# Where the weights of half-token products begin: one place, or six in turn

## The chip, the cores and the metric

The kernel runs on one core of a Trainium2 chip. The metric is the device time of one execution in microseconds; of several runs the median counts.

## The reference

Two decoder layers over 512 tokens of width 1024, all in float32. What matters here is the MLP that ends each layer and the gemms around it:

```python
def hybrid_layer(x, g_mix, w_in, sinks, w_a, w_b, w_out, g_mlp, w_up, w_down):
    h = rmsnorm(x, g_mix)
    z = h @ w_in                      # q, k, v, retention and gate columns
    ...                               # windowed attention and retention
    mixed = jax.nn.sigmoid(ga) * ya + jax.nn.sigmoid(gb) * yb
    x = x + mixed @ w_out
    h2 = rmsnorm(x, g_mlp)
    x = x + jnp.square(jax.nn.relu(h2 @ w_up)) @ w_down      # D_FF = 4096
    return x

def reference(x, ...):
    for l in range(DEPTH):            # DEPTH = 2
        x = hybrid_layer(x, ...)
    return rmsnorm(x, g_final)
```

## The kernel before, in words

Everything is kept transposed: features on the 128 partitions, tokens along the free dimension. Each float32 operand is split in two rounded parts, high and low, and each product of a weight block with an activation tile is three matmuls that accumulate in PSUM (`products`, L282 to L284): high weights on high activations, high weights on low activations, low weights on high activations. The weights are the stationary operand, a block of 128 x 128; the activations are the moving operand, 512 columns for all the tokens or 256 for half of them. Each matmul has a weight load of its own, so the same high block is loaded twice.

The weights come from HBM in units of 128 x 1024 floats (eight blocks of 128 columns), in an order written out by hand (`unit_order`). `split_until` takes the next unit, has ScalarE round it to the high part (L237) and VectorE subtract to get the low part (L238), both into rotating buffers of the pool `wpool`, three deep. `unit` hands out a unit and keeps the splitting three units ahead. A buffer is 1024 + 128 floats long, that is 4608 bytes or nine times 512, so all buffers begin at the same remainder of 512 bytes, and so do the activation tiles. A weight block is 512 bytes per partition.

Most gemms use all 512 tokens. Two parts use half the tokens:

- The `pair` steps of the up projection. Two chunks of 128 features are computed together by a scheme of seven products in place of eight (the blocks are halves of the contraction and halves of the tokens). A pair has four parts, which VectorE forms by adding and subtracting halves of the loaded weights (`add_part`); seven calls of `multiply` then do four blocks each on 256 columns. There are 14 pairs per layer, and their entry in the order is `("pair", j, part)` with j = 4, 6, ... 30. Between two pairs stands a `down` step: two output chunks of the down projection over all 512 tokens. A layer's sequence is `first`, two pairs, then twelve times down and pair, then `last`.
- The last gemm of the second layer (`end`), which goes twice over the same eight units of `w_down`, once per half of the tokens. The first three units come from `wpool`; the last five are split into `homes`, tiles of the slots named r, where they begin at the start of the tile.

The profile names operands by tile: a matmul `mm<-r,hi` has the moving operand r and the weights hi; `mm<-r,r` and `mm<-uhi,r` of 256 columns are the matmuls of `end` with weights in `homes`.

For units of half-token products (the pairs, and the last eight units of all) the weights begin `ASIDE` = 48 floats into the buffer, which is 192 bytes; for all other units they begin at its start:

```python
first = ASIDE if paired or i >= len(order) - 8 else 0
hi, lo = (wpool.tile([P, UNIT + P], F32R, tag=n, name=n)[:, first : first + UNIT] for n in ("hi", "lo"))
```

Of the kernel before, what the change touches and what calls it, by code (L numbers as in the profile page):

```python
# [46 lines left out]
PACE = 0.8  # L47
DEEP = 3
DELAY = 2
ASIDE = 48  # L50


def unit_order():

    order = [("w_in", i) for i in range(4 + 2 + 8 + 2 + 4 + 2)]
    order += [("w_in", i) for i in range(22, 26)]
    order += [("w_a", i) for i in range(4)]
    order += [("w_in", i) for i in range(26, 42)]
    order += [("w_b", i) for i in range(4)]
    order += [("w_in", i) for i in range(42, 46)]  # L60
    order += [("w_b", i) for i in range(4, 8)]
    order += [("w_out", i) for i in range(8)]
    for what, q, i in mlp_sequence():
        if what == "first":
            order += [("w_up", u) for u in range(4)]
        elif what == "pair":
            order += [("pair", 8 * q + 2 * i, part) for part in range(4)]
        elif what == "down":
            order += [("w_down", 8 * q + 2 * i + u) for u in range(2)]
        else:  # L70
            order += [("w_down", 8 * q + u) for u in range(8)]
    return order
# [43 lines left out]
def decoder(ctx, tc, xT, x_first, w_in, w_a, w_b, w_out, w_up, w_down, tables, decay, band, out):  # L116
# [11 lines left out]
    def f32(ap):  # L128
        return ap.bitcast(F32)
# [25 lines left out]
    order = [(layer, *u) for layer in range(DEPTH) for u in unit_order()]  # L155
# [3 lines left out]
    def halves(i):  # L159

        return (slice(0, UNIT // 2), slice(UNIT // 2, UNIT)) if i < 3 else (slice(0, UNIT),)
# [11 lines left out]
    def load_until(n):  # L173
        while state["loaded"] < min(n, len(order)):
            i = state["loaded"]
            layer, name, j = order[i][:3]
            if name == "pair":
                load_part(i)
            else:
                raws[i] = raw_tile()  # L180
                for at in halves(i):
                    queue = nc.scalar if i == 0 and at.start == 0 else nc.sync
                    queue.dma_start(raws[i][:, at], weights[name][layer, j][:, at])
                    if i < 3:
                        load_x()
            state["loaded"] += 1
# [17 lines left out]
    def add_part(i):  # L204
        part = order[i][3]
        if part == 0:
            w2 = raws[i + 3]
            nc.vector.tensor_tensor(raws[i][:, RIGHT], w2[:, RIGHT], w2[:, LEFT], ALU.add)
        elif part == 1:
            w1 = raws[i - 1]  # L210
            nc.vector.tensor_tensor(raws[i][:, LEFT], w1[:, RIGHT], w1[:, LEFT], ALU.subtract)
        elif part == 2:
            raws[i] = big("raw3").rearrange("p a t -> p (a t)")
            w1, w2, z2 = raws[i - 2], raws[i + 1], raws[i - 1]
            nc.vector.tensor_tensor(raws[i][:, LEFT], w1[:, LEFT], w2[:, RIGHT], ALU.subtract)
            nc.vector.tensor_tensor(raws[i][:, RIGHT], z2[:, RIGHT], z2[:, LEFT], ALU.subtract)

    def split_until(n):
        while state["split"] < min(n, len(order)):
            i = state["split"]  # L220
            load_until(i + 3)
            paired = order[i][1] == "pair"
            if paired:
                add_part(i)
            raw = raws[i]
            if homes and i >= len(order) - len(homes):
                home = homes[len(order) - 1 - i]
                hi, lo = (home[:, 2 * a : 2 * a + 2, :].rearrange("p a t -> p (a t)") for a in range(2))
            else:

                first = ASIDE if paired or i >= len(order) - 8 else 0
                hi, lo = (wpool.tile([P, UNIT + P], F32R, tag=n, name=n)[:, first : first + UNIT] for n in ("hi", "lo"))
            for at in (LEFT,) if paired and order[i][3] == 3 else halves(i):
                if i == 0 and at.start == 0:
                    nc.vector.tensor_copy(hi[:, at], raw[:, at])
                else:
                    nc.scalar.activation(hi[:, at], raw[:, at], AF.Copy)  # L237
                nc.vector.tensor_tensor(lo[:, at], raw[:, at], f32(hi[:, at]), ALU.subtract)  # L238
            raws.pop(i - 3 if paired else i, None)
            parts[i] = (hi, lo)  # L240
            state["split"] += 1

    def unit(name, layer):
        i = state["next"]
        assert order[i][:2] == (layer, name), (order[i], layer, name)
        state["next"] += 1
        split_until(i + 3)
        return parts.pop(i)
# [851 lines left out]

    scaled_input(0, 0)
    split_until(1)
    for u in (2, 3):
        for k in (2 * u - 3, 2 * u - 2):
            scaled_input(k, 0)
        split_until(u)
# [149 lines left out]
```

## Time and profile before

| | |
|---|---|
| median of 3 runs | 1505.11 us (1504.9 to 1505.15) |
| the profiled execution | 1507.24 us |
| its span, first to last instruction | 1505.5 us |
| mean granted TensorE clock | 0.998 |
| matmuls, TensorE busy | 8080, 1493.5 us (99%) |
| weight loads, busy | 8080, 1297.2 us (86%) |
| VectorE, ScalarE busy | 1026.4 us (68%), 740.1 us (49%) |
| HBM traffic over the span | 100 GB/s |

The half-token stages lie at 436 to 710 us (pairs of the first layer, with the down steps between them), 1178 to 1438 us (pairs of the second layer) and 1438 us to the end (`end`). A row of the groups of instructions reads: line, engine, operation, out<-in, stationary size, shape and count | busy us, mean ns of one | idle time before. A row of the timeline reads: start us, length us, engine, line, operation. The duration of a matmul holds the latency of the pipeline; matmuls overlap, so the step from one start to the next is shorter than a duration.

### The profile page before, as it was taken

The page shows a single profiled execution, that of the slowest core. Times are in us where ns is not written, and L with a number is a line of the kernel's source. Part 1 is how long each engine was busy: PE and PEld are TensorE (multiplying, and loading weights), DVE is VectorE, ACT ScalarE, POOL GpSimd, SP SyncE. Part 2 cuts the span into 40 slices and gives each one's busy share as a digit, 9 for nine tenths or more (in the row PEclk, how much of TensorE's full clock was granted, in tenths as well). Part 3 has the DMA queues.
Part 4 walks back from the last instruction along what each step waited for, and adds up shares of the span by engine and source line. Part 5 has one row for each costly group of instructions (what it writes and reads, how often), then busy time and mean ns, then how long its engine had stood idle before and what let it go on. Part 6 is the DMA issues. An engine that isn't in the chain of part 4 may idle for free.

```text
span 1505.5 us, 20498 instructions
## 1 busy us (share of the span) xinstructions
PE 1493.5 (99%) x8080; PEld 1297.2 (86%) x8080; DVE 1026.4 (68%) x1598; ACT 740.1 (49%) x1163; POOL 2.9 (0%) x13
## 2 busy tenths in 40 slices
PE   9999999999999999999999999999999999999997
PEld 7888888888888999989888888888888999899997
DVE  6877658754697666676678765677449866666664
ACT  6656455632564444444455643555226544444452
POOL 0000000000000000000000000000000000000000
PEclk9999999999999999999999999999999999999999
DMA  6322322233223232233442222222342222232231
GB/s 215 125 99 71 95 87 91 71 126 125 98 73 112 99 111 88 98 111 115 166 130 94 85 84 89 81 90 84 126 126 91 92 98 98 99 109 101 100 111 57
DMA packets 52640, 155.10 MB, mean 103 GB/s; under 512 B 6208, under 2 KB 8384, under 8 KB 52544
## 3 DMA queue, kind: packets, MB, share of 16 engines
q1 hardware_dynamic: 52400, 153.54, 30.5%
q8 instruction: 63, 1.03, 0.3%
q14 instruction: 33, 0.27, 0.1%
q10 hardware_dynamic: 144, 0.26, 0.0%
HBM read 146.96 MB, written 4.19 MB: 100 GB/s over the span
## 4 chain that ended last, share of the span: by engine, by line
PE 98%; ACT 1%; DVE 0%; DMA 0%; issue 0%; DVEq 0%
PE mm L284 29%; PE mm L282 29%; PE mm L283 29%; PE rv L282 2%; PE rv L284 2%; PE rv L283 2%; PE score L653 1%; PE pT L618 1%; PE r L283 1%; PE r L284 1%; PE r L282 1%; PE pv L639 0%; PE pv L638 0%; PE ssq L376 0%; PE ret L283 0%; PE ret L284 0%
## 5 line engine op out<-in xcount | busy, mean ns | idle before, releaser
L237 ACT ACTIVATE hi<-raw 128x1024 fp32r<-128x1024 f32 (+1 forms) x313 | 314.7, 1013 | 514.0 <-PE mm L283 430.7
L238 DVE TENSOR_TENSOR lo<-raw,hi 128x1024 fp32r<-128x1024 f32 (+1 forms) x314 | 362.6, 1164 | 161.7 <-ACT hi L237 160.7
L283 PE MATMUL mm<-r,hi 128*128 128x512 f32 (+1 forms) x1136 | 390.2, 344 | 0.0
L282 PE MATMUL mm<-r,hi 128*128 128x512 f32 (+1 forms) x1136 | 387.8, 345 | 1.1 <-ACT mm L1039 1.1
L284 PE MATMUL mm<-r,lo 128*128 128x512 f32 (+1 forms) x1136 | 386.7, 344 | 0.0
L282 PE MATMUL mm<-xh,hi 128*128 128x512 f32 (+1 forms) x1008 | 357.0, 356 | 0.6 <-ACT xh L292 0.6
L283 PE MATMUL mm<-xl,hi 128*128 128x512 f32 (+1 forms) x1008 | 355.5, 355 | 0.0
L284 PE MATMUL mm<-xh,lo 128*128 128x512 f32 (+1 forms) x1008 | 354.9, 355 | 0.0
L282 PEld LDWEIGHTS mm<-r,hi 128*128 128x128 f32 x1136 | 212.5, 187 | 27.6 <-ACT mm L1039 1.5
L283 PEld LDWEIGHTS mm<-r,hi 128*128 128x128 f32 x1136 | 213.3, 188 | 25.9
L284 PEld LDWEIGHTS mm<-r,lo 128*128 128x128 f32 x1136 | 213.1, 188 | 25.6
L282 PEld LDWEIGHTS mm<-xh,hi 128*128 128x128 f32 x1008 | 189.8, 188 | 26.7 <-ACT xh L292 1.3
L283 PEld LDWEIGHTS mm<-xl,hi 128*128 128x128 f32 x1008 | 190.1, 189 | 25.5
L284 PEld LDWEIGHTS mm<-xh,lo 128*128 128x128 f32 x1008 | 189.9, 188 | 25.6
L1066 DVE TENSOR_TENSOR x<-x,mm 128x512 f32<-128x512 f32 x56 | 37.8, 687 | 33.7 <-PE mm L284 33.7
L284 PE MATMUL rv<-hi,xl 128*128 128x512 f32 x128 | 49.8, 389 | 0.0
L283 PE MATMUL rv<-lo,xh 128*128 128x512 f32 x128 | 49.8, 389 | 0.0
L282 PE MATMUL rv<-hi,xh 128*128 128x512 f32 x128 | 49.4, 391 | 0.0
L283 PE MATMUL mm<-ulo,hi 128*128 128x512 f32 (+1 forms) x128 | 46.1, 362 | 0.0
L282 PE MATMUL mm<-uhi,hi 128*128 128x512 f32 (+1 forms) x128 | 46.1, 362 | 0.0
L284 PE MATMUL mm<-uhi,lo 128*128 128x512 f32 (+1 forms) x128 | 45.5, 363 | 0.0
L1046 DVE SCALAR_TENSOR_TENSOR z<-mm,rstd 128x256 f32<-128x256 f32 x28 | 11.9, 425 | 40.2 <-PE mm L284 40.2
(188 smaller groups left out, 1681.6 us busy)
## 6 DMA issues: line engine op xcount, KB each, us to landing
raw<-w_in_in SPq DMA_DIRECT2D x89, 512.0 KB, 3.3
raw<-w_down_in SPq DMA_DIRECT2D x64, 512.0 KB, 3.3
raw<-w_up_in SPq DMA_DIRECT2D x36, 512.0 KB, 3.3
raw<-w_up_in SPq DMA_DIRECT2D x56, 256.0 KB, 2.8
raw<-w_b_in SPq DMA_DIRECT2D x16, 512.0 KB, 3.2
raw<-w_out_in SPq DMA_DIRECT2D x16, 512.0 KB, 3.6
raw<-w_a_in SPq DMA_DIRECT2D x8, 512.0 KB, 3.3
x<-xT_in SPq DMA_DIRECT2D x15, 256.0 KB, 3.7
```

What stands on the lines that cost most here:

```text
L237: nc.scalar.activation(hi[:, at], raw[:, at], AF.Copy)
L238: nc.vector.tensor_tensor(lo[:, at], raw[:, at], f32(hi[:, at]), ALU.subtract)
L282: nc.tensor.matmul(ps, ah, bh, start=start and i == 0, stop=False, **more)
L283: nc.tensor.matmul(ps, ah, bl, start=False, stop=False, **more)
L284: nc.tensor.matmul(ps, al, bh, start=False, stop=stop and i == n - 1, **more)
L618: nc.tensor.transpose(pt[:, i * P : (i + 1) * P], sm[:, at : at + P], ident)
L653: nc.tensor.matmul(ps[:, g * w : (g + 1) * w], q_s[g][:, c, at], part[:, keys], start=i == 0, stop=i == 1)
L1046: nc.vector.scalar_tensor_tensor(z[:, 0, :H], a, 0.0, rms_mlp.value[:, :H], ALU.max, ALU.mult)
L1066: nc.vector.tensor_tensor(x[:, c, :], x[:, c, :], ps, ALU.add)
```

## The change

The one place of 48 floats becomes a list of six places, 16, 32, 64, 80, 96 and 112 floats (64, 128, 256, 320, 384 and 448 bytes). A pair takes the place by its number, j // 2 modulo six, and all four parts of a pair have the same place; each of the last units takes it by its own number. All other units still begin at the start of the buffer.

```diff
-ASIDE = 48
+ASIDE = (16, 32, 64, 80, 96, 112)
...
-                first = ASIDE if paired or i >= len(order) - 8 else 0
+
+                j = order[i][2]
+                first = ASIDE[(j // 2 if paired else j) % len(ASIDE)] if paired or i >= len(order) - 8 else 0
                 hi, lo = (wpool.tile([P, UNIT + P], F32R, tag=n, name=n)[:, first : first + UNIT] for n in ("hi", "lo"))
```

## The prediction

> **What bounds the kernel now.** I read the page first: its busy shares, then the chain of work that ended last.
>
> ```profile
> PE 1493.5 (99%) x8080; PEld 1297.2 (86%) x8080; DVE 1026.4 (68%) x1598; ACT 740.1 (49%) x1163; POOL 2.9 (0%) x13
> ...
> PE 98%; ACT 1%; DVE 0%; DMA 0%; issue 0%; DVEq 0%
> ```
>
> TensorE is the bound nearly everywhere: 98% of the chain is matmul after matmul. So the time is the number of matmuls times the step from one start to the next, and a change that touches only how a weight load reads its operand is worth what it does to that step. The groups of instructions, with shapes kept apart, come next, because matmuls of 256 columns (half the tokens) are what the change touches.
>
> ```profile
> L282 PE MATMUL mm<-xh,hi 128*128 128x512 f32 x672 | 263.3, 395 | 0.6 <-ACT xh L292 0.6
> ...
> L282 PE MATMUL mm<-r,hi 128*128 128x256 f32 x464 | 129.8, 280 | 1.1 <-ACT mm L1039 1.1
> ...
> L282 PE MATMUL mm<-xh,hi 128*128 128x256 f32 x336 | 93.8, 279 | 0.0
> ...
> L282 PE MATMUL mm<-r,r 128*128 128x256 f32 x48 | 13.6, 283 | 0.0
> ...
> L282 PE MATMUL mm<-uhi,r 128*128 128x256 f32 x32 | 9.1, 283 | 0.0
> ```
>
> The second name on the right is the stationary operand. Weights named "hi" of 256-column matmuls lie 48 floats (192 bytes) into their buffer; weights named "r" are the five units of the last gemm that sit in the slot tiles, at a multiple of 512 bytes from the moving operand (place zero below). The first kind reads 279 to 280 ns, the second 283. The weight loads say the same:
>
> ```profile
> L282 PEld LDWEIGHTS mm<-r,hi 128*128 128x128 f32 x1136 | 212.5, 187 | 27.6 <-ACT mm L1039 1.5
> ...
> L282 PEld LDWEIGHTS mm<-r,r 128*128 128x128 f32 x48 | 9.2, 192 | 0.0
> ```
>
> A load takes 187 ns in one kind and 192 in the other. (The first row mixes half and full matmuls.) A duration holds the pipeline's latency, so the step has to be read from starts. The timeline of TensorE gives it for one uninterrupted stretch of each kind, and the groups in the same stretch give the counts:
>
> ```profile
> 469.22 0.28 PE L282 MATMUL mm<-r,hi 128*128 128x256 f32 x1
> ...
> 476.17 0.28 PE L284 MATMUL mm<-r,lo 128*128 128x256 f32 x1
> ...
> L282 PE MATMUL mm<-r,hi 128*128 128x256 f32 x12 | 3.3, 279 | 0.0
> L283 PE MATMUL mm<-r,hi 128*128 128x256 f32 x12 | 3.3, 279 | 0.0
> L284 PE MATMUL mm<-r,lo 128*128 128x256 f32 x11 | 3.1, 280 | 0.0
> L284 PE MATMUL mm<-xh,lo 128*128 128x256 f32 x8 | 2.2, 280 | 0.0
> L282 PE MATMUL mm<-xh,hi 128*128 128x256 f32 x8 | 2.2, 279 | 0.0
> L283 PE MATMUL mm<-xl,hi 128*128 128x256 f32 x8 | 2.2, 279 | 0.0
> ```
>
> The groups (taken up to 476.1) hold 59 matmuls before the one at 476.17: 6.95 us / 59 = 117.8 ns a step with the weights at 192 bytes.
>
> ```profile
> 1460.73 0.28 PE L284 MATMUL mm<-uhi,r 128*128 128x256 f32 x1
> ...
> 1469.97 0.28 PE L283 MATMUL mm<-ulo,r 128*128 128x256 f32 x1
> ...
> L284 PE MATMUL mm<-uhi,r 128*128 128x256 f32 x14 | 4.0, 283 | 0.0
> L282 PE MATMUL mm<-uhi,r 128*128 128x256 f32 x14 | 4.0, 283 | 0.0
> L283 PE MATMUL mm<-ulo,r 128*128 128x256 f32 x14 | 4.0, 283 | 0.0
> L282 PE MATMUL mm<-r,r 128*128 128x256 f32 x12 | 3.4, 283 | 0.0
> L283 PE MATMUL mm<-r,r 128*128 128x256 f32 x12 | 3.4, 283 | 0.0
> L284 PE MATMUL mm<-r,r 128*128 128x256 f32 x12 | 3.4, 283 | 0.0
> ```
>
> Here 78 matmuls, 77 steps: 9.24 us / 77 = 120.0 ns at place zero. The place of the weights is thus worth 2.2 ns a step between the two places that the trace shows. A third value stands where the last gemm goes from place zero back to weights at 192 bytes:
>
> ```profile
> 1471.17 0.28 PE L284 MATMUL mm<-r,r 128*128 128x256 f32 x1
> 1471.29 0.28 PE L282 MATMUL mm<-r,hi 128*128 128x256 f32 x1
> ...
> 1472.20 0.28 PE L284 MATMUL mm<-r,lo 128*128 128x256 f32 x1
> ...
> L282 PE MATMUL mm<-r,hi 128*128 128x256 f32 x3 | 0.8, 276 | 0.0
> ```
>
> From 1471.29 to 1472.20 are eight steps, 0.91 / 8 = 113.8 ns (the starts are rounded to 10 ns, so 1 ns either way), and these matmuls read 276 ns. The same place has a quicker rhythm than the usual one, and it ended only when another product came between. So there are at least three rhythms: 113.8, 117.8 and 120.0.
>
> **The change part by part.** Nothing is added, removed or moved: every engine issues the same instructions in the same order, and all buffers keep their addresses. What changes is the offset, within its buffer, of the weights of the products with half the tokens. A weight block of 128 floats is 512 bytes, and the moving operands start at multiples of 512 bytes from one another, so one number per unit (its place, 64 to 448 bytes) describes all its blocks.
>
> *Counts.* A pair does seven products of 4 blocks, three matmuls each: 84. There are 14 pairs a layer, numbered 2 to 15, and the number modulo six gives the place; the three buffered units of the last gemm have 2 x 24 matmuls each, at the first three places. That makes 384 at 64 bytes (4 pairs and a unit), 384 at 128, 552 at 256 (6 pairs and a unit), 504 at 320, 336 at 384 and 336 at 448: 2,496 matmuls, all on the path. None remains at 192 bytes.
>
> *The evacuations and splits.* ScalarE (L237) and VectorE (L238) write the units to the new places. The row of L237 in the half-token stage (436 to 710 us, 192 bytes for nearly all) and in the stage ahead of it (250 to 430 us, place zero):
>
> ```profile
> L237 ACT ACTIVATE hi<-raw 128x1024 fp32r<-128x1024 f32 x66 | 68.7, 1058 | 108.7 <-PE mm L283 108.7
> ...
> L237 ACT ACTIVATE hi<-raw 128x1024 fp32r<-128x1024 f32 x31 | 32.8, 1060 | 71.7 <-PE mm L283 54.4 <-issue 17.3
> ...
> 436.00:710.00 274.00, 273.44 (x1765) 249.64 (x1764) 187.58 (x256) 127.33 (x183) 0.96 (x1) 1.00 0.31 104
> ```
>
> 1058 against 1060 ns: the writer does not mind the place, and it waits 108.7 us for TensorE in that stage. I cost this at nothing; the cover is that wait. In the stretch's own row (busy us of PE, PEld, DVE, ACT, POOL, then clock, DMA share) VectorE has 187.58 of 274 us and the DMA engines 0.31, so even 4 ns less a step (3%) makes neither late. The granted clock is 1.00.
>
> *The steps.* Each place costs its matmuls times the difference of its step from 117.8. The trace shows no weights at the six places, so I bound them by its rows: all at 120.0 gives 2,496 x 2.2 = +5.5 us; all at 113.8 gives 2,496 x -4.0 = -10.0 us; all as 192 bytes gives 0. Nothing excludes an end. What I take: the rows show that 120.0 is what the usual layout gives, at two sorts of moving operand and for 9 us on end, and 192 bytes the one place that has escaped it, and that with a margin of only 2.2 ns. I read it as an exception with a width. Its neighbours at 128 and 256 bytes get half the relief: (384 + 552) x 1.1 = 1.0 us. The other four, 384 + 504 + 336 + 336 = 1,560 matmuls, fall back to 120.0: 1,560 x 2.2 = 3.4 us. Sum: +4.5 us. The edges between half and full products (two or so at each of 28 pairs) would at 2.2 ns each add 0.1 us, which I leave out.
>
> [...]
>
> The profiled execution ran 1507.24 us, with a span of 1505.5; 1.7 us lie around the span, and the change leaves those alone. Its sum is 1507.2 + 4.5 = 1511.7. The median of the three runs is 1505.11, 2.1 us below the profiled one, and the steps are the same in kind, so the forecast goes by the median: 1505.1 + 4.5 = 1509.6 us.
>
> **The rivals.**
> *Several places keep the quick rhythm (faster).* [...] For it: the nine matmuls at 1471.29 held it until interrupted. Against: in the stretch at 469.22, entered from full matmuls as every pair is, the same place ran 117.8 from end to end. A place is worth on the mean 416 matmuls x 4.0 = 1.7 us; with two quick and the rest at 117.8 it is -3.3 us (1501.8), three -5.0 (1500.1), all six -10.0 (1495.1). It decides for faster when the mean step falls below 116.6 ns (3.0 us / 2,496 = 1.2 ns).
>
> *The place matters only when it is zero, or by halves (no change).* If only equal starts collide, all six run as 192 bytes does: 1505.1. If only the places nearer to a multiple of 512 than to 192 (64, 384, 448 bytes: 1,056 matmuls) fall back, it is +2.3 us (1507.4). For it: just one bad place is on show. Against: just one better place is, too.
>
> *Worse than zero.* Places close to a multiple of 512 could cost more than zero itself. The nearest dearer row of that shape:
>
> ```profile
> L282 PE MATMUL r<-r,r 128*128 128x256 f32 x16 | 4.6, 290 | 0.0
> ```
>
> That is 7 ns over 283. At 64 and 448 bytes, 720 matmuls x 7 = 5.0 us more: 1514.6. Against: those are short products between others of other lengths, not a steady stream.
>
> **How the numbers follow.** The forecast, +3.3 (six tenths of the matmuls at 120.0) to +5.5 us, has 0.42; worse than zero 0.08; no change or halves 0.25; quick places 0.25. Only the first is my likeliest and gives 1509.6, its own range 1508.4 to 1510.6. With 0.2% being 3.0 us, about what a measurement of this kernel can tell from no change: slower 0.50, same 0.25, faster 0.25. For 8 in 10 the range goes up past all places at 120.0 to 1511.5, leaving most of the dearest case out (0.06), and down to 1500.5, which holds the cases of no change and of two quick places and leaves out three and more (0.13).
>
> **What would show it.** In the profile after, the 256-column matmuls of "hi" and "lo" should read 283 ns and their loads 192 in the pairs at 64, 320, 384 and 448 bytes, and something between in the others; the timeline within a pair should step by 120.0. L237 and L238 stay at their durations and the full matmuls at theirs. The forecast is wrong if pairs at those places read 279 ns (no change) or 276 (faster), or if the pairs do not differ by their number at all; and the mechanism is wrong if the time moves while the 256-column rows do not.

## The result and the profile after

The changed kernel runs 1510.77 us (median of 6 runs), the kernel before 1505.13 beside it: a ratio of 1.0028, 95% interval 1.0017 to 1.0038. The profiled execution took 1511.14 us. One thing has to be known to read single times of this kernel: its first matmuls step by 427 ns and later ones by 227, and how long that lasts differs from run to run, which moves a run by an estimated 2 us (last section), so steps are read from the trace.

The page of the kernel after, span, busy time and the chain that ended last:

```profile
span 1509.4 us, 20498 instructions
...
PE 1497.0 (99%) x8080; PEld 1299.8 (86%) x8080; DVE 1026.3 (68%) x1598; ACT 739.9 (49%) x1163; POOL 2.9 (0%) x13
...
PE 98%; ACT 1%; DVE 0%; DMA 0%; issue 0%; DVEq 0%
```

TensorE still carries 98% of the chain; VectorE and ScalarE are unchanged (1026.4 and 740.1 us busy before, 1026.3 and 739.9 after). The groups of TensorE instructions with shapes kept apart (the lines have moved by two), and L239 of ScalarE, once L237, in the first pair stage:

```profile
L284 PE MATMUL mm<-r,hi 128*128 128x256 f32 x464 | 130.8, 282 | 1.0 <-ACT mm L1041 1.0
...
L284 PE MATMUL mm<-xh,hi 128*128 128x256 f32 x336 | 94.5, 281 | 0.0
...
L284 PE MATMUL mm<-r,r 128*128 128x256 f32 x48 | 13.6, 283 | 0.0
...
L239 ACT ACTIVATE hi<-raw 128x1024 fp32r<-128x1024 f32 x66 | 68.7, 1058 | 109.8 <-PE mm L285 108.0 <-DVE lo L240 1.8
```

The half-token matmuls with displaced weights went from 279 to 280 ns to 281 to 282; those at place zero kept 283; the writing kept 1058. But a mean over six places hides what happened. The timeline of TensorE, first and last matmul of the first six products of a pair (72 matmuls without a gap, so 71 steps), for pairs 5, 6, 7, 9, 10 and 14 of the first layer, which have 448, 64, 128, 320, 384 and 256 bytes:

```profile
489.10 0.28 PE L284 MATMUL mm<-xh,hi 128*128 128x256 f32 x1
497.46 0.28 PE L286 MATMUL mm<-r,lo 128*128 128x256 f32 x1
...
509.88 0.28 PE L284 MATMUL mm<-xh,hi 128*128 128x256 f32 x1
518.25 0.28 PE L286 MATMUL mm<-r,lo 128*128 128x256 f32 x1
...
530.72 0.29 PE L284 MATMUL mm<-xh,hi 128*128 128x256 f32 x1
539.24 0.29 PE L286 MATMUL mm<-r,lo 128*128 128x256 f32 x1
...
572.79 0.28 PE L284 MATMUL mm<-xh,hi 128*128 128x256 f32 x1
581.16 0.28 PE L286 MATMUL mm<-r,lo 128*128 128x256 f32 x1
...
593.63 0.29 PE L284 MATMUL mm<-xh,hi 128*128 128x256 f32 x1
602.15 0.29 PE L286 MATMUL mm<-r,lo 128*128 128x256 f32 x1
...
677.40 0.28 PE L284 MATMUL mm<-xh,hi 128*128 128x256 f32 x1
685.91 0.28 PE L286 MATMUL mm<-r,lo 128*128 128x256 f32 x1
```

Divided by 71: 117.7, 117.9, 120.0, 117.9, 120.0 and 119.9 ns. In these pairs odd multiples of 64 bytes (64, 320, 448, and 192 before) step by 117.8, even ones (128, 256, 384, and zero) by 120. How near a place lies to 192 bytes does not matter: 128 and 256, its neighbours, are dear.

Where the 3.9 us of span (1509.4 - 1505.5) came from, by summing the steps of all matmuls of both traces: the half-token matmuls 2.7 us (1,272 of them at even places, x 2.2 = 2.8), the full matmuls of the two pair stages 1.1, the rest 0.1. The 1.1 us lie where half and full matmuls meet. The timeline of the kernel before gives the first matmul of pairs 5 and 6:

```profile
488.59 0.28 PE L282 MATMUL mm<-xh,hi 128*128 128x256 f32 x1
...
509.38 0.28 PE L282 MATMUL mm<-xh,hi 128*128 128x256 f32 x1
```

From pair to pair that is 20.79 us. After, it is 20.78 behind pair 5 (448 bytes) but 20.84 behind pair 6 (509.88 to 530.72) and behind pair 9 (572.79 to 593.63), although these step by 117.9 as well: the way out of a pair at 64 or 320 bytes, and into the even place that follows here, costs 0.05 to 0.06 us more. Most of it belongs to 64 and 320 themselves: in the run of three odd places (below), where an odd place follows, pairs at 64 and 320 bytes take 20.82 to 20.83 us.

### The profile page after: what moved, and what is told of

It reads as the page before. It is cut to its first block, busy times and chain, and to the rows that moved or that the text cites. A ratio compares the mean times of both kernels' runs of the same rounds, so it can differ in the third digit from the quotient of the medians.

```text
span 1509.4 us, 20498 instructions
## 1 busy us (share of the span) xinstructions
PE 1497.0 (99%) x8080; PEld 1299.8 (86%) x8080; DVE 1026.3 (68%) x1598; ACT 739.9 (49%) x1163; POOL 2.9 (0%) x13
## 4 chain that ended last, share of the span: by engine, by line
PE 98%; ACT 1%; DVE 0%; DMA 0%; issue 0%; DVEq 0%
PE mm L284 29%; PE mm L285 29%; PE mm L286 29%; PE rv L284 2%; PE rv L286 2%; PE rv L285 2%; PE score L655 1%; PE pT L620 1%; PE r L286 1%; PE r L285 1%; PE r L284 1%; PE pv L641 0%; PE pv L640 0%; PE ssq L378 0%; PE ret L285 0%; PE ret L286 0%
## 5 line engine op out<-in xcount | busy, mean ns | idle before, releaser
L239 ACT ACTIVATE hi<-raw 128x1024 fp32r<-128x1024 f32 (+1 forms) x313 | 314.7, 1013 | 516.7 <-PE mm L285 429.7
```

## Experiments

All but one (the shift of all addresses) edit where the weights begin; the diffs with the list of six places are against the changed kernel, the others against the kernel before. The kernel before ran beside each.

**One even place for all.**

```diff
-ASIDE = (16, 32, 64, 80, 96, 112)
+ASIDE = (64,)
```

> All half-token weights at one place, 256 bytes. Theory A (what counts is the remainder of the distance between weights and moving operand modulo 128 bytes: odd multiples of 64 are good, even ones bad): the whole 2,496 matmuls step by 119.6 to 120.2 ns, so 2,496 x 1.8 to 2.4 = +4.5 to +6.0 us over the kernel before. Theory B (the prediction's: 192 bytes is an exception with a width, its neighbours get half): 2,496 x 1.1 = +2.7 us.

Measured: 1511.18 us against 1505.46, ratio 1.0039 (1.0027 to 1.0051). The timeline, pair 5 of the first layer:

```profile
486.96 0.28 PE L284 MATMUL mm<-xh,hi 128*128 128x256 f32 x1
...
495.47 0.28 PE L286 MATMUL mm<-r,lo 128*128 128x256 f32 x1
```

8.51 / 71 = 119.9 ns. As theory A says; the exception with a width (B), which asked for +2.7 us, is out.

**Three odd places in turn.**

```diff
-ASIDE = (16, 32, 64, 80, 96, 112)
+ASIDE = (16, 80, 112)
```

> The half-token weights take the three places 64, 320 and 448 bytes in turn. Theory A: every matmul steps by 117.7 to 117.9 ns as at 192 bytes; the time is that of the kernel before, up to +1 us for the edges to the full matmuls, which are dearer at 64 and 320 than at 448 bytes. Theory B: most at 120.0, +5.5 us.

Measured: 1506.43 against 1505.46, ratio 1.0003 (0.9994 to 1.0011): no difference, as A says. But behind a stall in each layer's first pair (in the kernel before TensorE idles there for 0.56 us in the first layer and 0.57 in the second) the stream is off the rule, as the timeline shows (72 matmuls; by the order of the program the first 12 are the last product of pair 2, at 448 bytes, the other 60 belong to pair 3, at 64 bytes):

```profile
446.33 0.28 PE L284 MATMUL mm<-r,hi 128*128 128x256 f32 x1
...
454.38 0.28 PE L286 MATMUL mm<-r,lo 128*128 128x256 f32 x1
```

8.05 / 71 = 113.4 ns: the quick rhythm, for as long as a whole pair. The matmuls of pair 2 behind its stall, at 448 bytes, already run so (from 439.56 to 444.67 us 45 steps of about 113 ns), and no full matmul comes between. So the odd places have two rhythms, and something other than the place chooses.

**Finer places**, between multiples of 64 bytes.

```diff
-ASIDE = (16, 32, 64, 80, 96, 112)
+ASIDE = (4, 8, 12, 20, 24, 28)
```

> Six finer places in turn: 16, 32, 48, 80, 96 and 112 bytes. Theory A with whole blocks of 64 bytes (only the block in which the weights begin counts): 16 to 48 bytes step by 120, 80 to 112 by 117.8; about half of the matmuls dearer, +2.5 to +3.5 us. Rival C (a load that does not begin at a multiple of 64 bytes touches one block more): all six above 120, more than +5.5 us. Rival D (the value slides with the distance): steps between 117.8 and 120 that rise and fall with the place.

Measured: 1509.60 against 1505.46, ratio 1.0024 (1.0015 to 1.0033). The total is near what A with whole blocks expected, but the steps are not. Timeline, pair 5 (112 bytes) and pair 10 (96 bytes):

```profile
487.17 0.28 PE L284 MATMUL mm<-xh,hi 128*128 128x256 f32 x1
495.69 0.28 PE L286 MATMUL mm<-r,lo 128*128 128x256 f32 x1
...
591.79 0.28 PE L284 MATMUL mm<-xh,hi 128*128 128x256 f32 x1
600.13 0.28 PE L286 MATMUL mm<-r,lo 128*128 128x256 f32 x1
```

120.0 ns at 112 bytes and 117.5 at 96, where A wanted 117.8 for both. In the first layer from pair 4 on, the places 16, 32, 48, 80, 96 and 112 bytes step by 118.3, 118.3, 118.3, 118.6, 117.4 and 120.0 ns. The value neither depends on the block alone, nor exceeds 120 throughout (C), nor slides evenly (D). All three expectations fail at places that are no multiple of 64; the rule of odd and even holds for multiples of 64 alone.

**Every address 64 bytes further on.**

```diff
-    little_x = const.tile([P, P + KD * T], F32, name="x")
+    little_x = const.tile([P, 16 + P + KD * T], F32, name="x")[:, 16:]
```

> The kernel before with every tile 64 bytes further on, so that all addresses change parity in steps of 64 bytes while the distance between half-token weights and moving operand stays 192 bytes. Theory A (the distance counts): the pairs step by 117.8 ns, as before. Rival G (the address of the weights itself counts): the pairs step by 120, +5.5 us, and the last gemm's units at the tile's start by 117.8.

Measured: 1504.77 in one run, before 1504.90. The timeline, pair 5:

```profile
486.08 0.28 PE L282 MATMUL mm<-xh,hi 128*128 128x256 f32 x1
...
494.44 0.28 PE L284 MATMUL mm<-r,lo 128*128 128x256 f32 x1
```

117.7 ns; and the last gemm's units at the tile's start still step by 120.0. For this shift it is the distance between stationary and moving operand that counts, not the address of the weights; rival G is out.

**Another odd place, 448 bytes**, for all half-token weights of the kernel before.

```diff
-ASIDE = 48
+ASIDE = 112
```

> All half-token weights at 448 bytes, another odd place, the one that had the cheapest edges in the run of three odd places. Theory A: 117.8 ns throughout, the time of the kernel before. Theory H: the same behind full matmuls, but the second part of each layer's first pair and its second pair, which follow a stall and no full matmul, at 113.3: about -0.4 us a layer, -0.8 us in all.

Measured: 1506.05 against 1504.90, ratio 1.0003 (0.9993 to 1.0012), all pairs at 117.8, those behind the stall too. The gain that theory H (the phase in which the stream ahead hands over chooses the rhythm; the next experiment tells where it came from) hoped for there did not come. In the run of three odd places the same matmuls behind the stall of pair 2, at the same 448 bytes, stepped by about 113: the place did not choose there either.

**All units displaced**, full products too.

```diff
-                first = ASIDE if paired or i >= len(order) - 8 else 0
+                first = ASIDE
```

> The kernel before, but with all units, those of the full products too, at 192 bytes. Theory E (a weight load during a full matmul of 226.7 ns is hidden and its place does not matter): full steps stay at 226.7, the time within 1 us of the kernel before. Rival F (the full matmul during which the first weights at 192 bytes are loaded reads 225.8 ns in the kernel before, 0.9 less): all full matmuls with buffered weights step by 225.8, 3,500 to 4,300 x 0.9 = -3 to -4 us, and the dear steps behind each pair (232.5 and 230.8) go, another 0.5 us.

Measured: 1514.28 against 1505.46, ratio 1.0063 (1.0049 to 1.0076). Both theories fall: full matmuls with displaced weights became dearer, 229 ns on the mean in the down steps between the pairs (226.7 at place zero in the kernel before), in a turn of 226, 229 and 232. But the two layers of one and the same execution differ. Timeline, pair 5 of the first and of the second layer:

```profile
491.04 0.28 PE L282 MATMUL mm<-xh,hi 128*128 128x256 f32 x1
499.40 0.28 PE L284 MATMUL mm<-r,lo 128*128 128x256 f32 x1
...
1238.81 0.28 PE L282 MATMUL mm<-xh,hi 128*128 128x256 f32 x1
1246.86 0.28 PE L284 MATMUL mm<-r,lo 128*128 128x256 f32 x1
```

117.7 and 113.4 ns, with the same code and places. The groups just ahead of those two pairs hold one full matmul, the last of the down step:

```profile
L284 PE MATMUL mm<-r,lo 128*128 128x512 f32 x1 | 0.4, 388 | 0.0
...
L284 PE MATMUL mm<-r,lo 128*128 128x512 f32 x1 | 0.4, 394 | 0.0
```

388 in the first layer, 394 in the second, at each of the later pairs too. From these two lengths the author took the turn of three to hand over at a different point, which no run shows by itself. This made theory H: the phase at the entry chooses the rhythm.

**Down steps displaced too.**

```diff
-first = ASIDE if paired or i >= len(order) - 8 else 0
+first = ASIDE if paired or i >= len(order) - 8 or (order[i][1] == "w_down" and order[i][2] < 24) else 0
```

> The kernel before with the units of the down steps between the pairs at 192 bytes too. Theory H (the rhythm of a pair is set by the phase in which the full matmuls ahead of it hand over; behind full matmuls that step 226, 229, 232 in turn a pair can enter at 113.3 and keeps it): in at least one layer twelve pairs step by 113.3; a pair gains 84 x 4.4 = 0.37 us and a down step loses 48 x 2.3 = 0.11 us, so -3 us for one layer, -6 us for both. Theory A alone (place fixes the step): pairs at 117.8, +2.5 us.

Measured: 1507.33 against 1504.90, ratio 1.0008 (0.9995 to 1.0021), but the eleven runs spread from 1499.00 to 1509.92, with 1502.68 and 1503.73 between. The profiled one (1507.39) has all pairs at 117.8. That one program spreads 11 us, of which the start can account for about 2, fits a choice made anew in each execution; no quick run of it was profiled.

**24 combinations in one kernel.**

```diff
+COMBO = [(f, p) for p in (16, 48, 80, 112) for f in (16, 32, 48, 80, 96, 112)]
...
-first = ASIDE if paired or i >= len(order) - 8 else 0
+layer, name, j = order[i][:3]
+step = j // 2 - 4 if paired else j // 2 if name == "w_down" and j < 24 else -1
+first = COMBO[12 * layer + step][0 if name == "w_down" else 1] if step >= 0 else ASIDE if paired or i >= len(order) - 8 else 0
```

> One look at 24 combinations: the units of the down step ahead of a pair at 64, 128, 192, 320, 384 or 448 bytes, the pair's own at 64, 192 (first layer), 320 or 448 (second layer). Theory H: pairs at one and the same odd place step by 113.3 behind some down steps and by 117.8 behind others. Theory A alone: all 24 pairs step by 117.7 to 117.9.

Measured: 1508.31 in one run. Timeline, pair 7 (64 bytes) and pair 13 (192 bytes), both behind a down step at 320 bytes:

```profile
529.95 0.28 PE L285 MATMUL mm<-xh,hi 128*128 128x256 f32 x1
538.00 0.28 PE L287 MATMUL mm<-r,lo 128*128 128x256 f32 x1
...
654.97 0.28 PE L285 MATMUL mm<-xh,hi 128*128 128x256 f32 x1
663.33 0.28 PE L287 MATMUL mm<-r,lo 128*128 128x256 f32 x1
```

113.4 and 117.7 ns. All twelve pairs at 64 and 320 bytes were quick, all twelve at 192 and 448 were not, whatever the down step. That looked like a rule of the place after all (H').

**Pairs at 64, down steps at 192 bytes.**

```diff
-first = ASIDE if paired or i >= len(order) - 8 else 0
+name, j = order[i][1:3]
+first = 16 if paired else ASIDE if i >= len(order) - 8 or (name == "w_down" and j < 24) else 0
```

> The kernel before with all pairs at 64 bytes and the units of the down steps between them at 192 bytes. Theory H' (behind full matmuls whose weights are displaced, a pair at 64 or 320 bytes enters the quick rhythm and keeps it, a pair at 192 or 448 does not): 24 pairs step by 113.3 and gain 84 x 4.4 = 0.37 us each, the 24 down steps lose 48 x 2.3 = 0.11 us each: -6.2 us. Theory H (the phase is a matter of history, not of the place): some runs quick, others not, as with the down steps and pairs both at 192 bytes. Theory A alone: +2.5 us.

Measured: 1505.45 against 1504.86, ratio 0.9987 (0.9977 to 0.9998); five runs between 1498.96 and 1502.19, six between 1505.45 and 1506.29. The profiled execution (1501.31) has every pair but the start of each layer's first one quick. H' promised that for each run; by the times the rhythm comes and goes, as H says. No execution at 1505 us or more was profiled.

**Pairs at 320, and the gemm ahead displaced too.**

```diff
-first = ASIDE if paired or i >= len(order) - 8 else 0
+name, j = order[i][1:3]
+first = 80 if paired else ASIDE if i >= len(order) - 8 or (name == "w_down" and j < 24) or (name == "w_up" and j < 4) else 0
```

> Pairs at 320 bytes, down steps between them at 192, and the four units of the gemm ahead of the first pair of each layer at 192 too. Theory H': 24 pairs quick as with 64 bytes, and with the displaced gemm ahead the first pair up to its stall as well; its 192 full matmuls lose 2.3 ns each, 0.4 us, and a third of a pair gains 0.1: -5.8 us. Theory H: some runs quick, others not.

Measured: 1501.64 against 1504.86, ratio 0.9975 (0.9966 to 0.9985), runs from 1499.18 to 1506.50. In the profiled execution (1506.50) the two layers differ again. The timeline, pair 5 of each layer, and the last full matmul ahead of it:

```profile
487.60 0.28 PE L283 MATMUL mm<-xh,hi 128*128 128x256 f32 x1
495.96 0.28 PE L285 MATMUL mm<-r,lo 128*128 128x256 f32 x1
...
1232.57 0.28 PE L283 MATMUL mm<-xh,hi 128*128 128x256 f32 x1
1240.62 0.28 PE L285 MATMUL mm<-r,lo 128*128 128x256 f32 x1
...
L285 PE MATMUL mm<-r,lo 128*128 128x512 f32 x1 | 0.4, 398 | 0.0
...
L285 PE MATMUL mm<-r,lo 128*128 128x512 f32 x1 | 0.4, 394 | 0.0
```

117.7 and 113.4 ns at the same 320 bytes, which speaks against H'. The slow layer's full matmuls drag too: the down steps ahead of its pairs step by 233 ns without a turn of three, those of the second layer by 229 in turn. Here the slow pairs follow a last full matmul of 398 ns, so its length alone does not tell which rhythm comes.

**Only the second unit of a down step displaced**, pairs at 64 bytes.

```diff
-first = ASIDE if paired or i >= len(order) - 8 else 0
+name, j = order[i][1:3]
+first = 16 if paired else ASIDE if i >= len(order) - 8 or (name == "w_down" and j < 24 and j % 2) else 0
```

> As the kernel with pairs at 64 and down steps at 192 bytes, but with only the second of a down step's two units displaced. Theory H' with the entry alone deciding: pairs at 113.3, the loss of the full matmuls halved to 24 x 2.3: -7.5 us. If the phase needs the whole down step: pairs at 117.8, +1.3 us.

Measured: 1498.58 against 1504.86, ratio 0.9957 (0.9945 to 0.9969), all five runs between 1498.37 and 1499.97. The timeline, pair 5:

```profile
485.76 0.28 PE L283 MATMUL mm<-xh,hi 128*128 128x256 f32 x1
...
493.81 0.28 PE L285 MATMUL mm<-r,lo 128*128 128x256 f32 x1
```

113.4 ns, and by the times in every run.

**The same with the pairs back at 192 bytes.** This tells the pair's place from the unit ahead of it.

```diff
-first = ASIDE if paired or i >= len(order) - 8 else 0
+name, j = order[i][1:3]
+first = ASIDE if paired else ASIDE if i >= len(order) - 8 or (name == "w_down" and j < 24 and j % 2) else 0
```

> The kernel with only the second unit of each down step displaced, but the pairs back at 192 bytes: tells whether the quick rhythm came from the pairs' place or from the displaced unit ahead of them. Theory H' (behind displaced full matmuls a pair needs 64 modulo 256 bytes): pairs at 117.8 in all or nearly all runs, +1.3 us over the kernel before. If the displaced unit alone does it: 113.3, about -6 us, as with the pairs at 64 bytes. Theory H: some runs quick, others not.

Measured: 1498.49 against 1505.07, ratio 0.9956 (0.9940 to 0.9973), four runs between 1498.28 and 1499.18. The timeline, pair 5 of each layer, then the groups around the first, with the last full matmul:

```profile
486.66 0.28 PE L283 MATMUL mm<-xh,hi 128*128 128x256 f32 x1
494.71 0.28 PE L285 MATMUL mm<-r,lo 128*128 128x256 f32 x1
...
1225.74 0.28 PE L283 MATMUL mm<-xh,hi 128*128 128x256 f32 x1
1233.78 0.28 PE L285 MATMUL mm<-r,lo 128*128 128x256 f32 x1
...
L283 PE MATMUL mm<-xh,hi 128*128 128x256 f32 x12 | 3.3, 276 | 0.0
...
L285 PE MATMUL mm<-r,lo 128*128 128x512 f32 x1 | 0.4, 394 | 0.0
```

113.4 and 113.2 ns (the same within the rounding) at 192 bytes, the place at which all pairs of the kernel before ran 117.8; all 24 pairs behind a down step run so. So H' is wrong: at 64 and at 192 bytes (113.4 ns both) the displaced unit ahead makes the rhythm. That it does so by the phase of entry is argued, from the two layers of one execution above; the last full matmul reads 394 here as in those quick layers. At place zero no quick rhythm was seen: in the last gemm of this run the quick stretch goes straight over into weights at place zero, and from 1449.06 us on these step by 120.0. Even places behind displaced full matmuls were not run. Why these two kernels are steady where the one with the whole down step displaced is not was not measured by itself. What differs is that the first unit of each down step, at place zero, comes between (its full matmuls step by 226 to 227), which would clear the phase before each turn of three; that is an argument, not shown.

These last two beat both kernels of the case, by 6 to 7 us against the kernel before and by 10 to 12 against the changed one, which did not run beside them.

## Why the prediction was right, and where not

- *The bound, and what the change touches: right.* Only the half-token weights moved, the writing engines kept their durations (ScalarE 1058 ns, VectorE 1223 in the first pair stage, before and after), and the time followed the step of the 256-column matmuls and its edges.
- *The two prices, 117.8 and 120.0: right.* In the pairs shown all six places fell on one of them, within 0.2 ns.
- *Which place has which price: wrong.* The step that failed is "I read it as an exception with a width". Four places were to fall back to 120.0 and two to go half way. In fact 64, 320 and 448 bytes keep 117.8, and 128 and 256, the neighbours, pay in full. By the prediction's own signs too: of the four places that should have read 283 ns only 384 bytes does (284), 64 and 320 read 281 and 448 reads 279. The two rows of before (zero and 192) could not tell an exception from an alternation, and the alternation was not among the rivals.
- *The sum: near by luck, through errors that partly cancel.* Three places did not fall back, 1,224 matmuls x 2.2 = 2.7 us too much; the two neighbours paid in full, 936 x 1.1 = 1.0 too little; so the steps gave +2.7 in place of 4.5. The edges, left out at 0.1, gave 1.1. Together with 0.1 elsewhere that is the 3.9 of the spans, whose two profiles start alike (20 matmuls in the window of the last section in both). The medians differ by 5.6 and the ratio of 1.0028 is 4.2 us. By their times, four of the six runs before have a short start and four of the six after a long one, which by estimate would add about 2 us to the difference of the medians.
- *The rival "quick places": did not come here.* In the changed kernel the pairs shown above ran in the two slower rhythms. Yet the reason given against it, that a pair enters from full matmuls, was not enough: behind full matmuls with displaced weights a pair ran quick at the same place (113.4 ns at 192 bytes in the last experiment).

## What to carry over

In this kernel a matmul's step hung on the distance of its two operands in SBUF: with 256 columns and a weight load for each matmul, even multiples of 64 bytes cost 120 ns a step and odd ones 117.8, and moving all addresses together by 64 bytes changed nothing (117.7). But at odd places a quicker rhythm of 113.3 ns was open as well, and what ran just before picked one (by its phase, as is argued above and not shown), so read the step pair by pair and run by run, and test a quick trace with several runs before it is believed. From two points of an unknown dependence, an alternation deserves to be a rival as much as a slope does.

## What was not expected of the hardware

- Three steady rhythms of a 256-column matmul with its own weight load at multiples of 64 bytes: 113.3, 117.8 and 120 ns, at the same mean granted clock (0.998). Why odd and even distances differ stays open; no run here shows it.
- The step of a full matmul, whose weight load reads 188 ns, less than the step, hung on the place of its weights too: 226 to 227 ns at place zero; at 192 bytes 229 on the mean, and in one layer 233.
- The start. The windows 4 to 12 us of the kernel before and of the last experiment (busy us and number of matmuls, clock, DMA share, GB/s):

```profile
4.00:12.00 8.00, 7.42 (x20) 1.00 1.01 369
...
4.00:12.00 8.00, 6.50 (x28) 1.00 1.01 374
```

  20 matmuls against 28 in the same 8 us: eight more full ones at 227 ns are 1.8 us. At first the steps read 427 ns, later 227; in the kernel before the last step of 427 ns starts at 9.85 us. The run with all addresses shifted (1504.77 us) begins its first pair at 433.71 us, the profiled one of the kernel before (1507.24) at 436.23: their whole difference lies ahead of it. Why the first matmuls step by 427 ns, and why their number differs, no run here shows: the clock column reads 1.00 in both windows.
